# Second MLP by seven products of 256 tokens for eight, with weight sums made in HBM: one change to a hybrid SSD / HGRN2 trunk

## The chip, the cores and the metric

The kernel runs on one core of a Trainium2 chip. Its time is the device time of one launch in microseconds (us), and the median of three runs is what counts. Engines are named as the profile names them: PE (TensorE matmuls), PEld (its weight loads), DVE (VectorE), ACT (ScalarE), POOL (GpSimd) and SP (SyncE). Each engine works through its own instruction queue in order.

## What is computed

Two layers over 512 tokens of width 1024, all in float32. Layer 0 mixes tokens by a Mamba-2 SSD, layer 1 by HGRN2. Behind each mixer stand a layer norm, an MLP with a squared ReLU and 4096 hidden units, a second layer norm and a gate on a per-layer input:

```
x = layer_norm(alpha * x + mixer(x))
h = square(relu(x @ w1))            # 512 x 1024 by 1024 x 4096
x = layer_norm(alpha * x + h @ w2)  # 512 x 4096 by 4096 x 1024
x = x + gate(x, p)
```

Only the MLP of layer 1 ("MLP 1") is computed in another way by the change. MLP 0, the gate of layer 0 and the HGRN stage between the two MLPs keep their arithmetic.

## The kernel before

Every float32 matmul is made of three: each operand is split into a high part in float32r and the rest, and `mm3` (L119 to L122) issues high by high, high by low and low by high. So each weight piece of 128 x 1024 goes through four steps: a DMA into `raw` (3 buffers) or `r` (8 buffers), a cast on ACT into `whi` (L113), a subtraction on DVE into `wlo` (L116), and 24 matmuls. `whi` and `wlo` have six buffers each. `unit()` does the first three steps for a piece from HBM, with SP issuing the load; `split()` does the cast and the subtraction for a piece that is in SBUF already.

The first half of an MLP makes 32 hidden tiles of 128 units by 512 tokens. `hidden(g)` makes 8 of them for each of four groups g: 24 matmuls of 128x512 into a bank `pj`, a ReLU from PSUM (L587) and a square (L589) on ACT. After each four tiles `half_blocks` makes seven operand blocks (`b8`, `blk`: four blocks and four signed sums) by adds on DVE, casts on ACT (L307) and subtractions on DVE (L308).

The second half is already done by seven products for eight (Strassen's scheme in Winograd's form): `block_product` cuts a group's part of w2 into 2 x 2 blocks, and each `product` is 24 matmuls of 128x512, first those of one bank (c = 0), then those of the other. The banks are `py` (two) and `pj`, and each is drained into `acc` by DVE (L377). Four of the seven products use sums of weight blocks. `weight_sums` makes them in SBUF: eight loads on POOL's queue (L329) and eight DVE adds of 128x1024 (L336, L339, L340, L344) for each group. In the last group of an MLP the products go p1, p7, p6, p4, p5, p2, p3, and the layer norm of each 128 tokens follows on its last drain.

`PERIODS` orders tiles (T) and products (Q); the tile framework's scheduler then sets the order of each engine's queue from priorities and its own estimates. `SUMS` is how far ahead of their place in the program the loads and adds of weight sums are ranked. The stage behind MLP 0 and its gate ("values", 740 to 790 us) uses `weight_sums` as well, with the same `r` buffers. `last_gate` at the end uses four more sums in `r`.

Of the kernel before, what the change touches and what calls it, by code (L numbers as in the profile page):

```python
# [15 lines left out]
P = 128  # L16
# [15 lines left out]
PERIODS = ("TTTTTTTT",) + 3 * ("TTQTQTQTQTQTQTQ",) + ("QQQQQQQ",)  # L32
SUMS = (60, 300, 300, 300)
# [11 lines left out]
def trunk(ctx: ExitStack, tc, a):  # L45
# [30 lines left out]
    bufs = dict(ssd=dict(two, xs=4, sz=4, y=2, xdt=2, ecs=2, ss=2), mlp0=mlp, hgrn=dict(two, xs=4, sz=4, cv=4, y=2, pv=2, btok=2, sc=2, scb=2, qd=2), mlp1=mlp)  # L76
# [149 lines left out]
    turned_last = []  # L226

# [3 lines left out]
    def transpose_split(src, dst, c, apart, keep=None):  # L231

        sl = slice(c * P, (c + 1) * P)
        for q in range(2):
# [50 lines left out]
    def norm(i, keep=None):  # L285
# [9 lines left out]
        return h_s, chunk, lambda c: transpose_split(acc[:, c, :], h_s, c, c == 3 and i % 2 == 0, keep), sums  # L295
# [4 lines left out]
    def half_blocks(blk, z0, z1, p):  # L300
# [11 lines left out]
        nc.vector.tensor_add(a22, a21, a22)  # L312
        put("a12", a12)
        nc.vector.tensor_sub(a21, a11, a21)
        nc.vector.tensor_sub(a11, a22, a11)
        nc.vector.tensor_sub(a12, a12, a11)
# [30 lines left out]
    def block_product(w, blk, lead, first, after=None, turns=None, sums=None, low=None):  # L347

        t1, t2, t3, t4 = weight_sums(w, lead, after=low)
# [3 lines left out]
        def product(x, f, name, start, i, j, turns=None):  # L355
            us = [split(v) if f in (t1, t2, t3, t4) else unit(v) for v in f]
# [3 lines left out]
            for c in range(2):  # L360
# [10 lines left out]
                with tc.high_priority(offset=SOON if after else 0):  # L371
                    if after and f in (w[1][0], t1, t4, w[1][1]):
                        nc.vector.tensor_tensor_reduce(
                            d, ps, d, 1.0, 0.0, ALU.add, ALU.add, sums[:, 2 - 2 * i + c, j : j + 1]
                        )
                    elif (i, j) in seen:
                        nc.vector.tensor_add(d, ps, d)  # L377
                    else:
                        nc.vector.scalar_tensor_tensor(d, d, ALPHA, ps, ALU.mult, ALU.add)
# [9 lines left out]
        for f in (p1, p7, p6, p4, p5, p2, p3) if after else (p1, p2, p6, p7, p5, p4, p3):  # L389
            f()  # L390
# [6 lines left out]
    def last_gate(wp, wg, h_s, p_s, kept, turned):  # L397

        t3, t1, t2, t4 = (tmp("r", [P, 1024]) for _ in range(4))
# [158 lines left out]
    def mlp_and_gate(layer, h_s, last):  # L558
# [5 lines left out]
        def hidden(g):  # L564
# [5 lines left out]
            for p in range(2):  # L570
                tiles = [4 * (2 * g + r) + 2 * p + i for r in range(2) for i in range(2)]
# [892 lines left out]
```

## Time and profile before

| | |
|---|---|
| time, three runs | 1413.84, 1412.04, 1412.05 us; median 1412.05 us |
| span of the profiled execution | 1409.6 us; its own time is not listed apart from the three runs |
| granted TensorE clock | 1.00 in every stage |
| SSD mixer | 0 to 380 us |
| MLP 0 and its gate | 380 to 740 us |
| values, HGRN and its output | 740 to 1020 us |
| MLP 1 and its gate | 1020 to 1410 us |

A row of the timeline reads: start in us, length in us, engine, line, operation, output<-inputs with buffer numbers left out, shapes, count; behind it in brackets the idle time of that engine ahead of the row and what ended it. A matmul's length is modelled and overlaps the next one; the step from start to start is what it costs. A row of the stages gives, for a stretch, the busy time of PE, PEld, DVE, ACT and POOL with their counts, the granted clock, the mean share of the 16 DMA engines in use, and GB/s.

### The profile page before, as it was taken

What the parts mean: (1) busy time and instruction counts of PE and PEld (TensorE: products, weight loads), DVE (VectorE), ACT (ScalarE), POOL (GpSimd) and SP (SyncE); (2) the same over time, 40 slices, a digit from 0 to 9 for tenths busy, and PEclk for the clock granted to TensorE, in tenths of its full rate; (3) what the DMA queues carried; (4) which work ended last, traced back from release to release, by engine and by line L of the source; (5) the groups of instructions that cost most, each with busy time, mean ns of one, the idle gap of its engine ahead of it and who ended that gap; (6) DMA issues with size and microseconds to landing.
All of it is one profiled execution on the core that took longest, in us unless ns stands there. A gap on an engine that the chain in (4) does not pass through costs nothing.

```text
span 1409.6 us, 20400 instructions
## 1 busy us (share of the span) xinstructions
PE 1404.3 (100%) x8001; PEld 1168.1 (83%) x8001; DVE 1069.1 (76%) x1778; ACT 763.6 (54%) x1156; POOL 45.8 (3%) x92
## 2 busy tenths in 40 slices
PE   9999999999999999999999999999999999999998
PEld 7888888888988888888888888888898888888887
DVE  7989688698977668677986577678785867667795
ACT  7766465573354444545555547655555454544573
POOL 0000000001000000000000000000100000000100
PEclk9999999999999999999999999999999999999999
DMA  8433333234433444345621421222443444444731
GB/s 313 135 117 120 106 120 110 85 100 156 141 113 127 157 131 152 129 142 178 209 90 49 134 91 61 76 87 96 150 135 105 147 137 148 144 137 159 202 106 60
DMA packets 50399, 181.69 MB, mean 129 GB/s; under 512 B 5632, under 2 KB 6400, under 8 KB 50176
## 3 DMA queue, kind: packets, MB, share of 16 engines
q1 hardware_dynamic: 38784, 138.45, 29.6%
q0 software_dynamic: 11520, 41.95, 9.2%
q8 instruction: 63, 1.03, 0.3%
q14 instruction: 32, 0.26, 0.1%
HBM read 177.16 MB, written 2.16 MB: 127 GB/s over the span
## 4 chain that ended last, share of the span: by engine, by line
PE 99%; DMA 0%; DVE 0%; issue 0%; DVEq 0%
PE pj L120 25%; PE pj L121 25%; PE pj L122 25%; PE py L120 5%; PE py L122 5%; PE py L121 5%; PE py L906 1%; PE pt L238 1%; PE py L1175 1%; PE pm L923 1%; PE pm L871 1%; PE py L1301 1%; PE pt L859 0%; PE py L1303 0%; PE py L1240 0%; PE py L832 0%
## 5 line engine op out<-in xcount | busy, mean ns | idle before, releaser
L113 ACT CAST whi<-raw 128x1024 fp32r<-128x1024 f32 x218 | 228.8, 1050 | 333.2 <-PE pj L121 243.6
L120 PE MATMUL pj<-b,whi 128*128 128x512 f32 (+1 forms) x990 | 378.6, 383 | 0.0
L122 PE MATMUL pj<-b,wlo 128*128 128x512 f32 (+1 forms) x990 | 376.8, 381 | 0.0
L121 PE MATMUL pj<-b,whi 128*128 128x512 f32 (+1 forms) x990 | 376.6, 381 | 0.0
L116 DVE TENSOR_TENSOR wlo<-raw,whi 128x1024 fp32r<-128x1024 f32 x218 | 265.4, 1221 | 129.4 <-ACT whi L113 128.2
L121 PEld LDWEIGHTS pj<-b,whi 128*128 128x128 f32 x990 | 186.4, 188 | 34.6 <-issue 0.9
L122 PEld LDWEIGHTS pj<-b,wlo 128*128 128x128 f32 x990 | 186.3, 188 | 34.5
L120 PEld LDWEIGHTS pj<-b,whi 128*128 128x128 f32 x990 | 186.1, 188 | 34.0
L122 PE MATMUL pj<-whi,b 128*128 128x512 f32 x520 | 204.1, 392 | 0.0
L120 PE MATMUL pj<-whi,b 128*128 128x512 f32 x508 | 202.1, 398 | 0.0
L121 PE MATMUL pj<-wlo,b 128*128 128x512 f32 x508 | 199.2, 392 | 0.0
L113 ACT CAST whi<-r 128x1024 fp32r<-128x1024 f32 x76 | 80.0, 1053 | 68.5 <-PE pj L122 39.4
L122 PEld LDWEIGHTS pj<-whi,b 128*128 128x128 f32 x520 | 97.7, 188 | 20.1
L120 PEld LDWEIGHTS pj<-whi,b 128*128 128x128 f32 x508 | 95.5, 188 | 19.1 <-ACT b L1322 0.3
L121 PEld LDWEIGHTS pj<-wlo,b 128*128 128x128 f32 x508 | 95.5, 188 | 18.7 <-issue 0.2
L116 DVE TENSOR_TENSOR wlo<-r,whi 128x1024 fp32r<-128x1024 f32 x76 | 92.5, 1220 | 19.6 <-ACT whi L113 19.1
L122 PE MATMUL py<-whi,b 128*128 128x512 f32 x260 | 101.3, 390 | 0.0
L121 PE MATMUL py<-wlo,b 128*128 128x512 f32 x248 | 96.6, 389 | 0.0
L120 PE MATMUL py<-whi,b 128*128 128x512 f32 x248 | 96.4, 390 | 0.0
L329 POOL DMA_DIRECT2D r<-in_w x64 | 34.0, 532 | 1098.8 <-DVE wlo L116 544.3
L122 PEld LDWEIGHTS py<-whi,b 128*128 128x128 f32 x260 | 48.8, 188 | 10.2
L800 DVE SCALAR_TENSOR_TENSOR cv<-pj,cst,cv 128x509 f32<-128x509 f32 (+2 forms) x66 | 48.9, 746 | 10.6 <-ACT cv L797 9.8
(368 smaller groups left out, 1943.5 us busy)
## 6 DMA issues: line engine op xcount, KB each, us to landing
raw<-in_w SPq DMA_DIRECT2D x112, 512.0 KB, 3.3
r<-in_w POOLq DMA_DIRECT2D x64, 512.0 KB, 3.8
raw<-in_wssd SPq DMA_DIRECT2D x36, 512.0 KB, 3.9
a<-csd SPq DMA_DIRECT2D x16, 512.0 KB, 4.1
raw<-in_wso SPq DMA_DIRECT2D x16, 512.0 KB, 3.3
raw<-in_whq SPq DMA_DIRECT2D x16, 512.0 KB, 3.4
raw<-in_wg SPq DMA_DIRECT2D x15, 512.0 KB, 4.0
raw<-in_whvg SPq DMA_DIRECT2D x14, 512.0 KB, 3.4
```

The lines of the kernel that those rows point to most:

```text
L113: nc.scalar.copy(hi[:, :n], f)
L116: nc.vector.tensor_sub(lo[:, :n], f, f32(hi[:, :n]))
L120: nc.tensor.matmul(out, sh, mh, start=start, stop=False, **kw)
L121: nc.tensor.matmul(out, sh, ml, start=False, stop=False, **kw)
L122: return nc.tensor.matmul(out, sl, mh, start=False, stop=stop, **kw)
L238: nc.tensor.transpose(pt[:, j * P : (j + 1) * P], src[:, k * P : (k + 1) * P], ident)
L329: queue.dma_start(t[i][u], src)
L800: nc.vector.scalar_tensor_tensor(cv[:, d:], ps[:, : T - d], convw[:, i, k : k + 1], cv[:, d:], ALU.mult, ALU.add)
L871: nc.tensor.matmul(pst_[:, c * P : (c + 1) * P], btok[:, c, :], xw[:, c].rearrange("p h q -> p (h q)"), start=True, stop=True)
L906: mm = nc.tensor.matmul(yds[0][64 * r : 64 * r + 64, sl], xdt[:, 2 * c + r, :], m[:, r, sl], start=True, stop=True)
L923: mm = nc.tensor.matmul(yo[:, c * P : (c + 1) * P], pv[:, c - 1].rearrange("p h q -> p (h q)"), cm[:, c * P : (c + 1) * P], start=True, st ...
L1175: nc.tensor.matmul(pcs[r][bs, at : at + n], kk[r][:, ts], qs, start=True, stop=True)
```

## The change

In the first half of MLP 1, 28 of the 32 tiles are made in 14 pairs, by the same scheme of seven products for eight. `pair()` does one: the 1024 inputs are cut in two halves, the two tiles are the two output halves, and the tokens are cut into 2 x 256. Each of the seven products is 12 matmuls of 128x256, so a pair takes 84 of them where two tiles took 48 of 128x512. The partial results go through PSUM into `z` by three copies on ACT and three adds on DVE, each 256 wide. The sums of the tokens are made once, by `token_sums`: four DVE adds, four ACT casts and four DVE subtractions of 128x1024, from a float32 copy `whole` that eight further ACT copies make while the layer norm's output is transposed. The four tiles made first stay as they were.

The sums of weight blocks, of w1 for the pairs and of w2 for MLP 1's second half, are formed in HBM ahead of time. `block_sums` lists 56 DMAs of 512 KB for s1 and 32 of 1 MB for s2, half of them copies from HBM to HBM and half of them adding copies, all on POOL's queue. `add_blocks` issues them during MLP 0 behind drains of `acc` and during HGRN behind matmuls ("pace"). In MLP 1 the 32 loads on POOL's queue and the 32 DVE adds are gone; the sums come by `unit` as plain weights do. A pair takes three and a half pieces of 128x1024 through load, cast and subtraction where two tiles took two. `PAIRS` orders the halves of products (q), products (Q) and parts of pairs (T); `last_gate` uses four buffers `tb` for its sums.

```diff
+PAIRS = ("TTTTTTTTTT",) + 3 * ("TTqqTTqqTqTTqqTqTqTqqTqTqq",) + ("QQQQQQQ",)
...
+    def block_sums():
...
+            yield small(o1, b21, False)
+            yield small(o3, b21, False)
+            yield small(o1, b22, True)
+            yield small(o3, b11, True)
+            yield small(o2, o1, False)
+            yield [(t1, wb, False)]
+            yield small(o2, b11, True)
...
+    def add_blocks(n=1):
+        for _ in range(n):
+            for out, src, add in next(steps, ()):
+                dma = nc.gpsimd.dma_start(out, src, **(dict(accum_op=ALU.add, max_dma_last_dim=8192) if add else {}))
+                tc.add_manual_dep(
+                    dma.ins, paced[0].ins.name, mybir.DependencyInfo(mybir.DependencyClass.Sync, mybir.DependencyReason.DATA), reason="pace"
+                )
...
+                if whole is not None:
+                    nc.scalar.copy(whole[c // 2][:, q, :, c % 2 * P : (c % 2 + 1) * P], v)
...
+    def pair(w1, q, h_s, ts, z, pz):
...
+        def product(ps, w, cs, x, start):
+            for k in range(4):
+                ks = slice(cs.start + k * P, cs.start + (k + 1) * P)
+                mm3(ps, w[0][:, ks], w[1][:, ks], *x(k), start and k == 0, k == 3, skip_group_check=True)
+        plain = unit(w1[2 * q])
+        product(xy[:, first], plain, low, part(0, first), True)
+        nc.scalar.copy(z[:, 0, first], xy[:, first])
+        product(zz[:, first], plain, high, part(4, first), True)
+        nc.vector.tensor_add(z[:, 0, first], zz[:, first], z[:, 0, first])
+        us = unit(both(0))
+        product(zz[:, second], us, low, ts[2], True)
+        nc.scalar.copy(z[:, 1, second], zz[:, second])
+        product(xy[:, first], us, high, ts[1], False)
+        nc.scalar.copy(z[:, 1, first], xy[:, first])
+        nc.scalar.activation(z[:, 0, first], z[:, 0, first], AF.Relu)
+        yield
...
+                if op == "Q" and not last and g < 4:
+                    add_blocks(2 if g > 1 else 1)
...
-                mm3(pss[c], *x, hi[:, ks], lo[:, ks], j + k == 0, j == 3 and k == 1)
+                paced[0] = mm3(pss[c], *x, hi[:, ks], lo[:, ks], j + k == 0, j == 3 and k == 1)
...
+    add_blocks(64)
+    whole = [mk(b8, [P, 2, 4, 256], "b8") for _ in range(2)]
+    h_s, *after = norm(2, whole=whole)
```

Up to the last group of MLP 0, and again from its gate to MLP 1, PE's matmuls stand in the same order as before, but for one place in the values stage and a few transposes of the norm between. The queues of the other engines move as follows. Lines of the kernel before and after differ: L329 is now L382, L336/L339/L340/L344 are L389/L392/L393/L397, L116 is L117, L377 is L435.

POOL, before: the eight loads of the sums of MLP 0's last group (`r_926` to `r_933`) stand right behind those of the group ahead of it.

```order
L329 DMA r_845_5012<-in_w2_0 128x1024 [waits DMASW6_49,DVE_49]
L329 DMA r_846_5013<-in_w2_0 128x1024 [waits DMASW7_49,DVE_49]
L329 DMA r_932_5543<-in_w2_0 128x1024 [waits DMASW0_49,DVE_49]
L329 DMA r_926_5537<-in_w2_0 128x1024 [waits DMASW1_49,DVE_49]
L329 DMA r_928_5539<-in_w2_0 128x1024 [waits DMASW2_49,DVE_49]
```

POOL, after, at the same loads: 21 DMAs of the sums stand between the two groups, of which these are the last.

```order
L270 DMA s2<-in_w2_1 16x16384 [waits DMASW5_49,DVE_49]
L270 DMA s1<-s1 128x2x512 [waits DMASW6_49,DMASW3_49]
L270 DMA s1<-s1 128x2x512 [waits DMASW7_49,DMASW4_49]
L382 DMA r_932_5589<-in_w2_0 128x1024 [waits Activation_49]
L382 DMA r_926_5583<-in_w2_0 128x1024 [waits Activation_49]
L382 DMA r_928_5585<-in_w2_0 128x1024 [waits DMASW2_49,Activation_49]
```

The loads now stand behind DMAs that wait for a drain on DVE and for one another.

DVE, before, at the end of MLP 0's third group: the adds into `r_926` to `r_933` stand 15 to 42 rows further up, and the first two subtractions from them are here, ahead of the last operand blocks.

```order
L116 TENSOR_TENSOR wlo_939_5571<-raw_937_5567,whi_938_5569 128x1024 [waits DMAHW2_49,Activation_49]
L308 TENSOR_TENSOR b8_828_4938<-b_857_5072,b8_828_4938 128x512 [waits Activation_49]
L377 TENSOR_TENSOR acc_2_99<-pj_888_5272,acc_2_99 128x512
L116 TENSOR_TENSOR wlo_943_5603<-r_926_5537,whi_942_5601 128x1024 [waits Activation_49]
L116 TENSOR_TENSOR wlo_945_5607<-r_927_5538,whi_944_5605 128x1024 [waits PE_49,Activation_49]
L377 TENSOR_TENSOR acc_2_99<-py0_855_5044,acc_2_99 128x512 [waits PE_49]
L308 TENSOR_TENSOR b8_827_4937<-b_897_5366,b8_827_4937 128x512 [waits Activation_49]
```

DVE, after, some ten rows later in its queue: `py1_941` is the second bank of the last group's first product p1, and `blk_830` (its next product, p7) is multiplied by the pieces `r_926` and `r_927`.

```order
L435 TENSOR_TENSOR acc_2_99<-py1_856_5071,acc_2_99 128x512
L736 TENSOR_TENSOR b_924_5578<-raw_925_5579,a_923_5577 128x1024 [waits DMAHW7_49,DVE_49,Activation_49]
L435 TENSOR_TENSOR acc_2_99<-py1_941_5620,acc_2_99 128x512 [waits PE_49]
L389 TENSOR_TENSOR r_926_5583<-r_926_5583,r_932_5589 128x1024 [waits DMASW1_49,DMASW0_49]
L392 TENSOR_TENSOR r_932_5589<-r_932_5589,r_928_5585 128x1024 [waits DMASW2_49,DVE_49]
L117 TENSOR_TENSOR wlo_943_5649<-r_926_5583,whi_942_5647 128x1024 [waits Activation_49]
L393 TENSOR_TENSOR r_928_5585<-r_926_5583,r_928_5585 128x1024 [waits DVE_49]
L389 TENSOR_TENSOR r_927_5584<-r_927_5584,r_933_5590 128x1024 [waits DMASW4_49,DMASW3_49]
```

All eight adds and the first four subtractions now stand behind the drain of p1's second bank.

DVE, before, in the values stage: `pt_1068` holds transposed outputs, and `py1_1069` the last bank of MLP 0's gate.

```order
L630 TENSOR_TENSOR b8_1003_5890<-pt_1068_6287,b8_1001_5888 128x4x128 [waits PE_49,Activation_49]
L116 TENSOR_TENSOR wlo_1097_6389<-raw_1095_6385,whi_1096_6387 128x1024 [waits DMAHW3_49,Activation_49]
L116 TENSOR_TENSOR wlo_1101_6429<-raw_1099_6425,whi_1100_6427 128x1024 [waits DMAHW4_49,Activation_49]
L116 TENSOR_TENSOR wlo_1104_6435<-raw_1102_6431,whi_1103_6433 128x1024 [waits DMAHW5_49,Activation_49]
L116 TENSOR_TENSOR wlo_1107_6470<-r_1073_6341,whi_1106_6468 128x1024 [waits Activation_49]
L116 TENSOR_TENSOR wlo_1109_6474<-r_1074_6342,whi_1108_6472 128x1024 [waits Activation_49]
L664 TENSOR_TENSOR sg_1071_6303<-py1_1069_6295,sg_1071_6303 128x512 [waits Activation_49]
```

DVE, after, at the same place: the last four of the stage's eight adds on `r` are seen here.

```order
L392 TENSOR_TENSOR r_1080_6394<-r_1080_6394,r_1076_6390 128x1024 [waits DMASW3_49,DVE_49]
L801 TENSOR_TENSOR acc_2_99<-sg_1067_6305,acc_2_99 128x512 [waits DVE_49]
L117 TENSOR_TENSOR wlo_1097_6435<-raw_1095_6431,whi_1096_6433 128x1024 [waits DMAHW3_49,Activation_49]
L117 TENSOR_TENSOR wlo_1101_6475<-raw_1099_6471,whi_1100_6473 128x1024 [waits DMAHW4_49,Activation_49]
L117 TENSOR_TENSOR wlo_1104_6481<-raw_1102_6477,whi_1103_6479 128x1024 [waits DMAHW5_49,Activation_49]
L393 TENSOR_TENSOR r_1076_6390<-r_1074_6388,r_1076_6390 128x1024 [waits DVE_49]
L397 TENSOR_TENSOR r_1077_6391<-r_1077_6391,r_1075_6389 128x1024 [waits DMASW4_49]
L397 TENSOR_TENSOR r_1078_6392<-r_1078_6392,r_1076_6390 128x1024 [waits DMASW5_49,DVE_49]
L765 TENSOR_TENSOR b8_1003_5936<-pt_1068_6333,b8_1001_5934 128x4x128
```

The read of `pt_1068`, which PE's next transposes wait for, and that of `py1_1069`, which the first matmuls of a product wait for, now stand behind these adds; seven adds were put between 748 and 763 us of the trace of before, and one ahead of that.

ACT, after, in MLP 1 where one group ends and the next begins: `b_1572` is the last `z` of the old group, `pj_1636` the first bank of the next pair.

```order
L672 ACTIVATE b_1572_10252<-pj_1601_10451 128x256 [waits PE_49]
L673 ACTIVATE b_1572_10252<-b_1572_10252 128x1024 [waits Activation_49]
L353 CAST b8_1514_9881<-b_1572_10252 128x512 [waits Activation_49]
L353 CAST b8_1513_9880<-b_1572_10252 128x512
L114 CAST whi_1651_10795<-raw_1650_10793 128x1024 [waits DMAHW1_49,PE_49]
L353 CAST b8_1515_9882<-b_1572_10252 128x512 [waits DVE_49]
L353 CAST blk_1518_9885<-b_1520_9887 128x512 [waits PE_49]
L353 CAST blk_1517_9884<-a_1571_10251 128x512 [waits DVE_49]
L114 CAST whi_1654_10801<-raw_1653_10799 128x1024 [waits DMAHW2_49]
L653 COPY a_1634_10685<-pj_1636_10687 128x256 [waits PE_49]
```

The copy of the next pair's first partial result, which PE must have before it adds to that bank, stands behind this work; before, a tile had no such copy.

More of the change, by code (lines that the diff above doesn't have):

```diff
@@ L283, in out_project, with norm @@
                     out_part(units, 4, xs, c, h, first, scale)
-    def norm(i, keep=None):
+    def norm(i, keep=None, whole=None):
         gb = ln_params(i)
@@ L293, in chunk, with half_blocks @@
                 layer_norm(i, c, gb, sums)
-        return h_s, chunk, lambda c: transpose_split(acc[:, c, :], h_s, c, c == 3 and i % 2 == 0, keep), sums
-    def half_blocks(blk, z0, z1, p):
+        return h_s, chunk, lambda c: transpose_split(acc[:, c, :], h_s, c, c == 3 and i % 2 == 0, keep, whole), sums
+    def half_blocks(blk, z0, z1, p, plus):
         ks = slice(2 * p, 2 * p + 2)
@@ L560, in mlp_and_gate @@
+    def mlp_and_gate(layer, h_s, last, whole=None):
         w1, w2 = a[f"w1_{layer}"], a[f"w2_{layer}"]
@@ L570, in hidden @@
             for p in range(2):
+                if whole is not None and (g or p):
+                    zs = [mk(w4, [P, 2, T], "ab"[r]) for r in range(2)]
+                    pairs = [pair(w1, 4 * g + 2 * r + p, h_s, ts, zs[r], ((pst, "pt"), (psm, "pm"))[r]) for r in range(2)]
+                    order = (0, 1, 0, 1, 0, 1) if g == 0 else (0, 0, 0, 1, 1, 1)
+                    for at, n in enumerate(order):
+                        next(pairs[n])
+                        if at == 5:
+                            half_blocks(blocks[g], *zs, p, True)
+                        yield
+                    continue
                 tiles = [4 * (2 * g + r) + 2 * p + i for r in range(2) for i in range(2)]
```

131 lines of the change are left out of this document (105 added, 26 removed).

## The prediction

> **What bounds the kernel now.** I read the page first, for the shares and the chain of waits.
>
> ```profile
> span 1409.6 us, 20400 instructions
> PE 1404.3 (100%) x8001; PEld 1168.1 (83%) x8001; DVE 1069.1 (76%) x1778; ACT 763.6 (54%) x1156; POOL 45.8 (3%) x92
> PE 99%; DMA 0%; DVE 0%; issue 0%; DVEq 0%
> ```
>
> PE is never idle and carries the whole chain, so a matmul saved is time saved, and any wait that is given to PE is time lost. The sum is made against the span of 1409.6 us; the median of the runs, 1412.05, is 2.45 us longer, and I add that at the end. The timeline of PE then gives what a matmul costs, by the steps from start to start, for 256 wide (first tiles of MLP 1) and 512 wide.
>
> ```profile
> 1025.75 0.28 PE L121 MATMUL pj<-b,whi 128*128 128x256 f32 x1
> ...
> 1027.43 0.28 PE L120 MATMUL pj<-b,whi 128*128 128x256 f32 x1
> 661.73 0.39 PE L120 MATMUL py<-whi,b 128*128 128x512 f32 x1
> ...
> 663.09 0.39 PE L120 MATMUL pj<-whi,blk 128*128 128x512 f32 x1
> ...
> 676.83 0.39 PE L120 MATMUL pj<-whi,b 128*128 128x512 f32 x1
> ```
>
> The first two are 14 steps apart: 0.120 us each. From 661.73 to 663.09 there are six: 0.227 us each. The last row is the spot at which MLP 0's last group has done its products p1, p7 and p6; I use it below. Third, the stages:
>
> ```profile
> 420.00:740.00 320.00, 320.00 (x1436) 264.66 (x1435) 241.82 (x298) 160.04 (x210) 16.95 (x32) 1.00 0.44 146
> 780.00:1020.00 240.00, 240.00 (x2236) 197.35 (x2235) 169.43 (x475) 141.34 (x318) 5.51 (x12) 1.00 0.31 102
> 1020.00:1060.00 40.00, 40.00 (x253) 36.14 (x252) 35.16 (x42) 22.86 (x35) 0.00 (x0) 1.00 0.38 122
> 1140.00:1220.00 80.00, 80.00 (x355) 66.26 (x354) 55.67 (x65) 38.14 (x48) 4.24 (x8) 1.00 0.45 144
> ```
>
> DVE is the next engine, with 70% in MLP 1's steady part and 88% at its start; DMA has room.
>
> **The gain.** Two tiles cost 48 x 0.227 = 10.90 us, a pair 84 x 0.120 = 10.08 us: 0.82 us saved, 14 times, 11.4 us. A product of half the width saves an eighth of the work and pays the part of a step that does not halve (0.120 against 0.1135) on all of it. The granted clock is 1.00 everywhere, so no stage owes a different step.
>
> For the same step the Trainium skill, "TensorE: Matmul & The Clock Gate", section "Back-to-back issue gap", gives N / 2.4 + 2.5 ns for the isolated gap, some 109 ns for 256 wide and 216 for 512; by that estimate a pair would save 1.19 us and all of them 16.6, and the sum below would be 5.2 us lower. The rows here disagree (120 and 227 ns), so I keep the rows.
>
> **MLP 0's last group: the largest loss.** PE's work there is not changed, but DVE's queue is. I walk it with these rows.
>
> ```profile
> 636.64 1.22 DVE L344 TENSOR_TENSOR r<-r,r 128x1024 f32<-128x1024 f32 x1 [0.23 <-DMA r<-in_w]
> 637.78 0.68 DVE L377 TENSOR_TENSOR acc<-py,acc 128x512 f32<-128x512 f32 x1
> 651.76 1.22 DVE L116 TENSOR_TENSOR wlo<-r,whi 128x1024 fp32r<-128x1024 f32 x1
> 655.99 1.22 DVE L116 TENSOR_TENSOR wlo<-r,whi 128x1024 fp32r<-128x1024 f32 x1 [3.01 <-ACT whi L113]
> 658.46 1.28 DVE L308 TENSOR_TENSOR b<-b,b 128x512 fp32r<-128x512 f32 x2
> 659.66 0.69 DVE L312 TENSOR_TENSOR b<-a,b 128x512 f32<-128x512 f32 x1
> 668.60 2.56 DVE L116 TENSOR_TENSOR wlo<-r,whi 128x1024 fp32r<-128x1024 f32 x2
> 671.07 0.68 DVE L377 TENSOR_TENSOR acc<-pj,acc 128x512 f32<-128x512 f32 x1
> ```
>
> Before, the last add was done at 637.8, the first subtractions from the sums ran at 651.8 and 656.0, and PE took the first at 663.09 and the second six matmuls later, at 664.45: 10 and 7 us in hand. A 512-wide operation costs 0.60 us (658.46 to 659.66 for two), a 1024-wide one 1.14 (636.64 to 637.78), or 1.24 with its wait (668.60 to 671.07 for two). In the changed queue fourteen 512-wide operations run from 658.46, and the last of them, the drain that frees p1's second bank, ends at 658.46 + 14 x 0.60 = 666.9. Before, PE filled that time with p7; now p1's second bank comes first, runs from 667.0 to 667.0 + 12 x 0.227 = 669.7, and its drain ends at 670.3. Only then come twelve 1024-wide operations, eight adds and four subtractions: 670.3 + 12 x 1.14 = 684.0. PE picks up each piece as it is made, and has 16 matmuls left behind the last: 684.0 + 16 x 0.227 = 687.6, against 676.83. That is 10.8 us. With 1.24 for each it is 12.0; if the first two pieces alone were late and the others overlapped (667.0 - 663.1 at the bank, 669.7 to 673.8 at the first piece), 8.0. I take 11, for the walk has all its rows from this very place, and keep 8 to 13. Behind it the two banks of the next products and the layer norm move along by the same time; nothing there waits for longer, since DVE is as late as PE is.
>
> The loads are not what costs: in the changed queue of POOL they wait for a drain at about 608 us and for eight DMAs of sums, which leaves 60 us until DVE wants them. The scheduler's place for the adds costs, and no cover is left, since p7 and p6 both use the sums.
>
> **The values stage.** The same eight adds come late a second time.
>
> ```profile
> 740.64 1.22 DVE L708 TENSOR_TENSOR blk<-blk,blk 128x1024 f32<-128x1024 f32 x1
> 745.99 0.69 DVE L664 TENSOR_TENSOR sg<-py,sg 128x512 f32<-128x512 f32 x1 [4.13 <-ACT sg L663]
> 747.93 1.22 DVE L682 TENSOR_TENSOR b<-blk,b 128x1024 fp32r<-128x1024 f32 x1
> 753.28 0.69 DVE L664 TENSOR_TENSOR sg<-py,sg 128x512 f32<-128x512 f32 x1 [4.14 <-ACT sg L663]
> 759.72 2.58 DVE L116 TENSOR_TENSOR wlo<-r,whi 128x1024 fp32r<-128x1024 f32 x2
> 762.22 0.69 DVE L664 TENSOR_TENSOR sg<-py,sg 128x512 f32<-128x512 f32 x1
> 762.96 0.50 PE L120 MATMUL py<-whi,b 128*128 128x512 f32 x1
> ```
>
> One add fits in the idle 4.13 us ahead of 745.99 and three in those ahead of 753.28. The other four have no cover: from 753.28 DVE has four 512-wide operations, four adds and five subtractions ahead of the gate's last read of PSUM: 753.28 + 4 x 0.60 + 9 x 1.14 = 765.9, where it ended at 762.9. PE's product at 762.96 waits for that read: 3.0 us, or 4.0 with 1.24 for each. I take 3.5, and keep 2 to 5 (a transposition ahead of it waits too, but inside the same time).
>
> **MLP 1.** Bytes and engines suffice. In a group of four pairs (78 us of PE) 30 pieces (four of them half as long) pass through `whi` and `wlo` instead of 22; DVE loses eight adds and gains six subtractions and twelve 256-wide adds, ACT six casts and twelve copies, which makes some 59 and 50 us of 78 (the stage's 55.67 and 38.14 of 80, with 0.4 for a 256-wide operation, an estimate from the 0.60 of 512). What shrinks is the time in hand: six `whi` buffers serve 30 uses in 78 us (15.7 us round) where they served 22 in 82 (22 us). The shortest way from a freed buffer to a weight ready for PE is a cast and a subtraction:
>
> ```profile
> 655.86 0.59 ACT L587 ACTIVATE b<-pj 128x512 f32<-128x512 f32 x1
> 656.48 1.07 ACT L589 ACTIVATE b<-b 128x1024 f32<-128x1024 f32 x1
> 657.58 1.14 ACT L307 CAST b<-b 128x512 fp32r<-128x512 f32 x2
> 667.49 1.05 ACT L113 CAST whi<-r 128x1024 fp32r<-128x1024 f32 x1
> ```
>
> 1.05 + 1.22 = 2.3 us, so inside a group I expect no wait. Where a group ends, ACT has a ReLU, a square, six casts of 512 (0.57 each) and two of 1024 ahead of the next pair's first copy: 0.4 + 1.1 + 6 x 0.57 + 2 x 1.05 = 7.0 us and some waits on DVE between, against 2 x 2.72 + 2 x 1.44 = 8.3 us of PE work: a wait of 0 to 1.5 us at the copy and as much at the next, three times. At the start, four token sums and four subtractions (8 x 1.14 = 9.1 us on DVE) take the place of eight adds, and each transposition waits for one more ACT copy of 0.57. No row of before shows this stage; from below it costs nothing (every piece in time), from above 15 us (three group ends at 3 us, and the start at 6, what its added copies, casts and subtractions come to beyond the idle 5 us of DVE there). I take 7, from the walk of the group ends (1.5 each) and 2.5 at the start.
>
> **Costed at nothing.** HGRN's order is unchanged; its PE order has the new semaphores, but no new wait. The DMAs of the sums move 61.9 MB beside its weight loads.
>
> ```profile
> q1 hardware_dynamic: 38784, 138.45, 29.6%
> q0 software_dynamic: 11520, 41.95, 9.2%
> raw<-in_w SPq DMA_DIRECT2D x112, 512.0 KB, 3.3
> ```
>
> 180.4 MB took 38.8% of the span, 330 GB/s while the engines run. The sums need 188 us at that rate, 281 if an adding DMA (half of them) counts twice for reading its target, in some 470 us from 526 on. That is 0.40 to 0.60 on top of 0.44 and 0.31. A load of 3.3 us may become two or three times as long; the weights have seven us and more in hand.
>
> **The sum.** -11.4 + 11 + 3.5 + 7 = +10.1: a span of 1419.7, a time of 1422.
>
> **The rivals.**
> - Faster: the walk of MLP 0's last group is too pessimistic, because the fourteen operations ahead of the drain start earlier or run beside one another, so that p7's first piece is late by only some 5 us and the rest follows in time; the values stage costs 2 and MLP 1 nothing. -11.4 + 5 + 2 = -4.4, 1407.7. It decides from the point where the three losses come to under 8.6. For it: DVE was idle for some 8 us between 641 and 658. Against it: the adds stand behind the drain of PE's own p1 in DVE's queue, which they can't pass.
> - No change: lower ends everywhere, 8 + 2 + 0 = 10, gives -1.4, 1410.7.
> - DMAs run full: with adds counted twice MLP 0's second half has 0.44 + 0.60 = 1.04. From a share over 1 on, weights come late: 4% of 470 us is 19 us more, 1441. For it: half of the sums are adds and each waits for the one ahead. Against it: HGRN has 0.31, and takes half of them. The Trainium skill, "DMA: Bandwidth & Descriptors", section "Issuing engines are not separate DMA queues", has all queues interleave on the same 16 engines, which is this rival's premise; no run so far shows both loads together.
> - The change doesn't do what it says: the pairs' steps are longer than 0.120 since a pair loads as many weights for half the columns. PEld is busy 83% now. If a step were 0.130, a pair would cost 10.92 and the gain would be gone: 1433. Against it: the first tiles of before do just this for 15 rows at 0.120.
>
> **Chances.** The forecast's own case (the three losses between 14 and 33, so a time of 1415 to 1434) 0.60; faster 0.19; no change 0.14; DMAs full 0.05; no gain 0.02. The range 1405 to 1434 leaves out the lower half of the faster case, the two last ones and what lies above the forecast's own. A measurement here tells 0.2%, 2.8 us, from no change: faster 0.19, same 0.14, and slower the other three, 0.67.
>
> **What would show it.** Right: PE rows of 128x256 stepping by 0.120 in MLP 1; PE idle behind DVE `wlo` and ACT `whi` at about 663 to 685 us for 11 us, and behind DVE at 760 to 767 for 3.5; single waits of about a us at three places in MLP 1. Wrong: no idle PE at 663 to 685, weights waiting for DMAs in HGRN, or waits all through MLP 1's groups, where I have none.

## The result, and the profile after

The changed kernel takes 1449.28 us (median of four runs, 1448.22 to 1453.77) against 1412.43 for the kernel before (four runs): a ratio of 1.0269, 95% interval 1.0252 to 1.0286. It is slower, as forecast, but by 37 us and not by 10; the time lies above the range. First the page of the profile after: span, engines, the chain of waits, and the two kinds of DMA queue (packets, MB, share of the 16 engines).

```profile
span 1446.6 us, 21844 instructions
PE 1412.2 (98%) x8505; PEld 1189.2 (82%) x8505; DVE 1082.4 (75%) x1824; ACT 806.1 (56%) x1252; POOL 104.7 (7%) x148
PE 41%; DVE 5%; DMA 5%; ACT 2%; issue 1%; ACTq 0%; DVEq 0%; SPq 0%
q1 hardware_dynamic: 47424, 166.24, 34.2%
q0 software_dynamic: 21376, 88.09, 24.3%
```

PE no longer carries the whole chain: DMA, DVE and ACT have entered it. (The chain is followed back to 667.6 us only; its shares are of the whole span and come to 54%. PE's busy time still reads 1412, in part since a matmul at a slower clock counts as busy for longer.) POOL's queue moves 88.09 MB in place of 41.95 and takes 24.3% of the engines' time in place of 9.2%. By stage (PE, PEld, DVE, ACT and POOL busy, granted clock, DMA share, GB/s):

```profile
580.00:640.00 60.00, 58.60 (x259) 48.19 (x258) 37.92 (x47) 29.73 (x39) 12.22 (x15) 1.00 0.91 237
640.00:700.00 60.00, 52.81 (x211) 41.88 (x210) 43.49 (x52) 23.69 (x29) 13.71 (x19) 0.91 0.96 278
700.00:760.00 60.00, 52.87 (x246) 42.75 (x245) 40.98 (x63) 29.54 (x51) 6.93 (x11) 0.94 0.80 247
900.00:1000.00 100.00, 100.00 (x1087) 82.53 (x1086) 72.13 (x229) 61.33 (x144) 20.69 (x24) 1.00 0.92 238
1140.00:1220.00 80.00, 79.78 (x505) 71.86 (x504) 59.76 (x78) 49.33 (x73) 0.00 (x0) 1.00 0.57 184
1300.00:1340.00 40.00, 37.58 (x214) 33.01 (x213) 24.29 (x31) 20.41 (x28) 3.49 (x5) 0.96 0.81 247
```

PE loses time where the engines' share is 0.91, 0.96 and 0.80 (MLP 0's end and its gate) and again past 1300, but none at 0.92 in HGRN: a full set of DMA engines costs nothing by itself. (Not for a share of 1 either: in single stretches of 6 us in HGRN it reads up to 1.20, from 966 to 972, and PE is busy throughout.) The waits of PE, largest first (us in total, how often, the longest):

```profile
PE pt L282 <- DVE acc L225: 7.5, 2, 5.9
PE py L121 <- DVE acc L435: 7.0, 5, 2.8
PE pj L121 <- ACT whi L114: 3.0, 1, 3.0
PE pj L121 <- DVE b L668: 2.4, 1, 2.4
PE py L121 <- DVE sg L799: 2.1, 1, 2.1
```

Next I set the start of each matmul beside that of the same one before (PE's order is the same but for a part of MLP 0's last group, a few transposes and MLP 1, where I count back from the end). How far the changed kernel is behind grows like this:

| stretch of the changed kernel | added, us | forecast |
|---|---|---|
| start | 0.5 | 0 |
| MLP 0's third group (at 594) | 1.7 | 0 |
| MLP 0's last group (660 to 695) | 12.4 | 11 |
| MLP 0's layer norm and gate (705 to 736) | 9.1 | 0 |
| values (786 to 794) | 5.4 | 3.5 |
| HGRN, then MLP 1 up to its last products, the gain included | 0.5 | -4.4 |
| last products and gate (from 1335) | 7.1 | 0 |
| sum | 36.7 | 10.1 |

**MLP 0's last group.** DVE's timeline follows the forecast's walk (the drain of p1's second bank forecast to end at 670.3, the adds from then to 684):

```profile
667.56 0.68 DVE L435 TENSOR_TENSOR acc<-py,acc 128x512 f32<-128x512 f32 x1
...
672.84 0.69 DVE L435 TENSOR_TENSOR acc<-py,acc 128x512 f32<-128x512 f32 x1 [3.46 <-PE py L123]
673.44 1.21 DVE L389 TENSOR_TENSOR r<-r,r 128x1024 f32<-128x1024 f32 x1
...
685.04 4.62 DVE L117 TENSOR_TENSOR wlo<-r,whi 128x1024 fp32r<-128x1024 f32 x4
```

The drain of p1's second bank ends at 673.44, and the adds stand behind it, as the order said. That is 3.1 us later than walked, of which 2.2 are the lag that the kernel brought along (0.5 and 1.7 in the table). The operations ahead of the drain ended some 1 us earlier than that, and the bank itself took 4.5 us (668.29 to 672.84) instead of 2.7. PE's rows show why:

```profile
668.29 0.80 PE L121 MATMUL py<-whi,b 128*128 128x512 f32 x1 [2.82 <-DVE acc L435]
668.89 0.63 PE L122 MATMUL py<-wlo,b 128*128 128x512 f32 x1
669.32 0.63 PE L123 MATMUL py<-whi,b 128*128 128x512 f32 x1
...
671.72 0.40 PE L123 MATMUL py<-whi,b 128*128 128x512 f32 x1
```

After a wait of 2.82 us the steps are 0.43 us instead of 0.227 for some 3 us, and then back to normal. The granted clock (the last number but two) says the same:

```profile
664.00:668.00 4.00, 1.48 (x7) 0.90 (x5) 4.00 (x8) 2.28 (x4) 0.00 (x0) 1.00 1.04 232
668.00:672.00 4.00, 3.71 (x10) 2.94 (x11) 1.37 (x2) 0.00 (x0) 0.00 (x0) 0.57 1.03 184
```

**The norm and the gate.** The chain of waits here names two loads of the gate's weights:

```profile
698.37 10.59 DMA raw<-in_wg
...
710.14 1.22 DVE wlo L117
...
715.79 9.63 DMA raw<-in_wp
...
726.58 1.23 DVE wlo L117
```

Before, such loads took 3.3 us (`in_wg`, median) and 4.3 (`in_wp`). DVE's subtraction of each stands ahead of layer-norm work in its queue, and PE's transposes wait for that (the 5.9 us at `pt`). DVE's timeline shows it for another such weight; L224 and L225 are the layer norm:

```profile
707.53 1.23 DVE L117 TENSOR_TENSOR wlo<-raw,whi 128x1024 fp32r<-128x1024 f32 x1 [4.53 <-ACT whi L114]
...
711.48 1.28 DVE L224 SCALAR_TENSOR_TENSOR acc<-acc,lnmv,a 128x1024 f32<-128x1024 f32 x1
...
717.55 2.47 DVE L225 SCALAR_TENSOR_TENSOR acc<-acc,lnrs,b 128x1024 f32<-128x1024 f32 x2
```

The cast at 706.45, for which DVE waits here, had itself kept ACT waiting 5.56 us for its load. Late weights hold up work that does not use them. The 1.7 us at 594 are of the same kind: DVE stands idle for 4.79 us, up to 587.48, for the cast of a late weight, and the drain that PE wants comes behind eight more operations.

**The end.** The chain from 1335, with a raw buffer's round of load, cast (ACT) and subtraction (DVE), three times over:

```profile
1335.65 6.22 DMA raw<-s
...
1341.89 1.07 ACT whi L114
...
1342.98 1.14 DVE wlo L117
...
1346.57 6.59 DMA raw<-s
...
1357.90 5.75 DMA raw<-s
```

The sums of the last group, which before stood ready in eight `r` buffers, now pass through three `raw` ones.

### The profile page after: what moved, and what is told of

Read it like the earlier page. It is cut to its first block, busy times and chain, and to the rows that moved or that the text cites. A ratio compares the mean times of both kernels' runs of the same rounds, so it can differ in the third digit from the quotient of the medians.

```text
span 1446.6 us, 21844 instructions
## 1 busy us (share of the span) xinstructions
PE 1412.2 (98%) x8505; PEld 1189.2 (82%) x8505; DVE 1082.4 (75%) x1824; ACT 806.1 (56%) x1252; POOL 104.7 (7%) x148
## 3 DMA queue, kind: packets, MB, share of 16 engines
q0 software_dynamic: 21376, 88.09, 24.3%
HBM read 251.09 MB, written 65.08 MB: 219 GB/s over the span
## 4 chain that ended last, share of the span: by engine, by line
PE 41%; DVE 5%; DMA 5%; ACT 2%; issue 1%; ACTq 0%; DVEq 0%; SPq 0%
PE pj L121 9%; PE pj L122 9%; PE pj L123 9%; PE py L121 2%; PE py L122 2%; PE py L123 2%; DVE wlo L117 2%; DMA raw<-s 2%; DMA raw<-in_w 1%; ACT whi L114 1%; DMA raw<-in_wg 1%; PE py L1310 1%; PE pt L121 1%; PE pm L121 1%; DMA raw<-in_wp 1%
## 5 line engine op out<-in xcount | busy, mean ns | idle before, releaser
L117 DVE TENSOR_TENSOR wlo<-raw,whi 128x1024 fp32r<-128x1024 f32 (+1 forms) x278 | 330.5, 1194 | 195.4 <-ACT whi L114 194.1
L114 ACT CAST whi<-raw 128x1024 fp32r<-128x1024 f32 (+1 forms) x278 | 285.2, 1028 | 319.6 <-PE pj L122 149.4
L121 PE MATMUL pj<-b,whi 128*128 128x512 f32 (+1 forms) x878 | 323.3, 369 | 3.1 <-DVE b L668 2.4
L122 PE MATMUL pj<-b,whi 128*128 128x512 f32 (+1 forms) x878 | 321.4, 366 | 0.0
L123 PE MATMUL pj<-b,wlo 128*128 128x512 f32 (+1 forms) x878 | 321.0, 366 | 0.0
L121 PEld LDWEIGHTS pj<-b,whi 128*128 128x128 f32 x878 | 165.5, 189 | 29.9 <-DVE b L668 2.8
L122 PEld LDWEIGHTS pj<-b,whi 128*128 128x128 f32 x878 | 165.9, 189 | 26.5 <-issue 0.9
L123 PEld LDWEIGHTS pj<-b,wlo 128*128 128x128 f32 x878 | 165.7, 189 | 25.8
L270 POOL DMA_DIRECT2D s<-in_w x66 | 61.1, 986 | 335.9 <-issue 149.0
L114 ACT CAST whi<-r 128x1024 fp32r<-128x1024 f32 x40 | 41.6, 1051 | 43.7 <-PE pj L123 18.4
L121 PEld LDWEIGHTS py<-whi,b 128*128 128x128 f32 x248 | 47.4, 191 | 20.8 <-DVE acc L435 9.1
L117 DVE TENSOR_TENSOR wlo<-r,whi 128x1024 fp32r<-128x1024 f32 x40 | 48.1, 1217 | 14.2 <-ACT whi L114 14.2
L123 PEld LDWEIGHTS py<-whi,b 128*128 128x128 f32 x260 | 49.5, 190 | 10.4
## 6 DMA issues: line engine op xcount, KB each, us to landing
s<-in_w POOLq DMA_DIRECT2D x16, 1024.0 KB, 11.9
```

The source lines that it names most:

```text
L114: nc.scalar.copy(hi[:, :n], f)
L117: nc.vector.tensor_sub(lo[:, :n], f, f32(hi[:, :n]))
L121: nc.tensor.matmul(out, sh, mh, start=start, stop=False, **kw)
L122: nc.tensor.matmul(out, sh, ml, start=False, stop=False, **kw)
L123: return nc.tensor.matmul(out, sl, mh, start=False, stop=stop, **kw)
L270: dma = nc.gpsimd.dma_start(out, src, **(dict(accum_op=ALU.add, max_dma_last_dim=8192) if add else {}))
```

## Experiments

My theory after the result: the sums' DMAs cost some 29 us, through their place in DVE's queue (12) and through full engines (the rest); the pairs themselves gain 11 in MLP 1 and lose as much in waits there, and the last products lose 7 for want of buffers. Rivals: the pairs cost more than they show; the order alone costs all of it; or the order costs nothing and only late loads do.

**1. The pairs without the sums' DMAs.** The 88 DMAs are left out, and MLP 1 reads plain pieces of w1 and w2 in the places of the sums.

```diff
-        for _ in range(n):
+        for _ in range(0):
...
-        both = lambda n: s1[q][:, n : n + 2, :].rearrange("p s n -> p (s n)")
+        both = lambda n: w1[2 * q + n // 2]
```

> The changed kernel without the 88 DMAs of the sums: MLP 1 reads plain pieces of w1 and w2 of the same sizes where it read sums, so its output is not the reference's. DVE's order up to MLP 1 is then that of the kernel before. My theory (36.8 us of loss = 29 between 590 and 790 us from the sums' DMAs, by DVE's late adds and by full DMA engines; 1 at HGRN's end; MLP 1 even, its gain of 11.2 eaten by small waits; 7 in the last products and the gate): the 29 go, 7 stay, 1420 us. Rival A (the last 7 are a late effect of the sums' DMAs too): 1413. Rival B (a part of the 29 comes from elsewhere, such as the clock): above 1425.

1418.61 us, ratio 1.0045 (1.0025 to 1.0064). 30.7 us of the 36.8 go with the DMAs. The lag is 1.35 up to HGRN and -1.7 where the last products begin, so the pairs do gain 3 us up to there; then the last products and the gate lose 8.9, where the changed kernel loses 7.1:

```profile
1290.00:1320.00 30.00, 23.95 (x121) 19.32 (x119) 15.93 (x21) 13.22 (x18) 4.83 (x7) 1.00 0.93 281
1310.48 6.61 DMA raw<-in_w
```

(A stage, and a row of its chain of waits.) So the end's loss belongs to MLP 1's own loads, and even with the sums for nothing the kernel is not faster.

**2. The sums' DMAs without the pairs.** The kernel before with the 88 DMAs and the same places for them; MLP 1 as it was.

> The kernel before with the 88 DMAs of the sums added at their places, MLP 1 as before (the sums are made and not used). DVE's order up to MLP 1 is that of the changed kernel. Theory: the loss up to HGRN alone, 29 us, so 1441 to 1442. Rival (the loss needs the pairs, for example their loads waiting for the sums): 1413 to 1420.

1445.08 us, ratio 1.0233 (1.0203 to 1.0263), 3 above the theory. The lag is 28.6 through HGRN (29.1 in the changed kernel), and grows by 6.7 behind it, mainly at two waits: 1.7 us from 1024 on, while sums still run, and 2.7 from 1133 on with a halved clock behind it. The second ends on an add of weight sums that stands late in DVE's queue, and the changed MLP 1 has no such adds. DMA shares in MLP 1's start, of this kernel:

```profile
1030.00:1060.00 30.00, 30.00 (x177) 25.60 (x176) 23.91 (x47) 14.44 (x31) 6.72 (x10) 1.00 0.86 229
1060.00:1090.00 30.00, 30.00 (x174) 26.49 (x173) 17.67 (x21) 17.99 (x26) 2.47 (x4) 1.00 0.91 288
```

The sums are not done when HGRN is; the last of them goes out at 1076 here and at 1069.65 in the changed kernel. I had not seen that: their chain, in which each adding DMA waits for the one ahead of it, runs over into MLP 1.

**3. The order alone.** The kernel before, with no DMA added; only the eight adds of weight sums of MLP 0's last group stand behind the drain of p1's second bank.

```diff
+            if defer and f is p1:
+                adds(drains[-1])
```

> The kernel before with one thing moved: the eight weight adds of MLP 0's last group stand behind the drain of the first product's second bank in DVE's queue, as in the changed kernel (all eight in a row, then the subtractions). No DMA is added, loads are where they were. Theory (the place in DVE's queue is enough): 11 to 16 us slower, 1424 to 1428, with PE idle between 665 and 690 us and half the clock for about 3 us behind each wait of some 3 us. Rival (that wait in the changed kernel came from loads landing late): 1412 to 1416.

1429.24 us, ratio 1.0121 (1.0091 to 1.015). A lag of some 16 us arises between 663 and 685 and nowhere else:

```profile
PE py L120 <- ACT whi L113: 3.3, 1, 3.3
PE pj L120 <- ACT whi L113: 3.0, 1, 3.0
640.00:700.00 60.00, 48.62 (x197) 38.36 (x196) 44.47 (x53) 23.70 (x28) 4.24 (x8) 0.89 0.42 149
```

(Two waits of PE, and the stage.) The engines' share is 0.42 there and no load is late, so the place in DVE's queue is enough for this term. It costs more than the 12.4 of the changed kernel: here all eight adds run ahead of the first subtraction, and there one subtraction runs after every two or three adds.

**4. The loads on the other queue.** The changed kernel, with the loads of `weight_sums` issued by SP instead of POOL. DVE's order becomes that of before up to MLP 1.

```diff
-    def weight_sums(w, lead, after=None, queue=nc.gpsimd):
+    def weight_sums(w, lead, after=None, queue=nc.sync):
```

> The changed kernel with the loads of weight sums of MLP 0 and of the values stage on SP's queue instead of POOL's, so that no DMA of s1 or s2 stands ahead of them; DVE's order up to MLP 1 is then that of the kernel before, the sums' DMAs stay. Theory (DVE's late adds cost 12.4 + 5.4 by themselves, full DMA engines 11): 1431. Rival (the DMA engines are full and everything that is loaded between 590 and 790 us is late whatever the queue): 1443 to 1449. Rival the other way (without the late adds nothing waits): 1421.

1463.16 us (two runs, 1457.93 and 1468.39), ratio 1.0361 (1.0273 to 1.0449): neither theory. The adds are back in their place, but their loads are not there. From the chain of waits:

```profile
649.64 12.53 DMA r<-in_w
668.18 11.15 DMA raw<-in_w
704.14 13.60 DMA raw<-in_w
```

Beside POOL's sums these loads take 11 to 14 us, though SP issues them, and in one queue `r` and `raw` hold each other up: from 600 to 720 SP's `r` loads wait 32 us in all for a buffer, with `raw` loads behind them. This agrees with the Trainium skill, "DMA: Bandwidth & Descriptors", section "Issuing engines are not separate DMA queues", by which another issuer saves only issue time. So mending the order doesn't help while the loads are late. The two runs also tell the causes apart at MLP 0's norm and gate: this one, with the order of before, loses 10.8 us there, and experiment 3, with late adds and no added DMA, loses nothing. The values stage, whose adds are back in their place, loses nothing here.

**5. The last group's sums in other buffers.** The eight pieces go, on POOL's queue, into the four token-sum buffers, free by then.

```diff
+                for t in (t3, t2, t4, t1):
+                    held.append(tmp("tb", [P, 2, 1024]))
+                    for u in range(2):
+                        nc.gpsimd.dma_start(held[-1][:, u], t[u])
```

> The changed kernel, but the eight pieces of weight sums of MLP 1's last group are loaded on POOL's queue into the four token-sum buffers, which are free by then, instead of passing through the three raw buffers on SP's queue. Same bytes, same casts and subtractions. Theory (at the end each raw buffer goes round load, cast, subtraction in about 8.5 us, 2.8 us for a piece against PE's 2.7, so the ring of three sets the pace): the 7.1 us lost in the last products and the gate shrink to 0 to 2, time 1442 to 1444. Rival (the DMA engines are the limit there, 0.8 busy, or the loads start too late): 1448 to 1450.

1445.48 us, ratio 1.0237 (1.0221 to 1.0252): 3.8 less. The end loses 0.9 instead of 7.1, so the way through the ring of three was its cause; but eight loads at once fill the engines just ahead of it (share 1.01), and PE waits 3.0 us and goes on at half the clock:

```profile
1330.00:1345.00 15.00, 12.01 (x64) 10.23 (x63) 7.81 (x9) 7.36 (x10) 2.12 (x4) 0.89 1.01 398
```

**6. A fourth raw buffer in MLP 1.**

```diff
+            raw = tmp("rx", [P, 1024]) if "rx" in phase[2] and turn[0] % 4 == 0 else mk(raws, [P, 1024], "raw")
```

> The changed kernel with a fourth raw buffer in MLP 1 and the last gate (every fourth piece goes into it; its room comes from the gate's two sigmoid buffers, which take token-sum buffers instead). Theory (three raw buffers are what holds MLP 1: SP waits for a raw buffer's subtraction 80 times, and 30 pieces a group pass through the three where there were 14, with eight r buffers beside them): 3 to 6 of the some 11 us of small waits in MLP 1 and 4 to 7 of the 7 us at the end go, time 1437 to 1443. Rival (the pace is set by ACT, DVE or the six whi buffers): within 2 of 1449.

1458.17 us (four runs, 1447.93 to 1460.91), ratio 1.0302 (1.026 to 1.0345): a miss, 9 slower in the median. The new buffer lies in the space of MLP 1, which HGRN's norm must leave first: its first load goes out at 1059.02, lands 9.85 us later, and its cast holds ACT for 6.52 us ahead of the norm's copies:

```profile
1068.89 1.04 ACT L117 CAST whi<-rx 128x1024 fp32r<-128x1024 f32 x1 [6.52 <-DMA rx<-in_w]
```

PE waits 8.3 us there, and the last products and the gate still lose some 6, by other waits. Whether a buffer that is free from the start would help stays open.

**7. No sums in MLP 0.** The DMAs go out behind SSD's projections and in HGRN.

```diff
-                if op == "Q" and not last and g < 4:
-                    add_blocks(2 if g > 1 else 1)
```

> The changed kernel, but none of the 88 DMAs of sums is issued in MLP 0: they go out behind projections of the SSD mixer (DMA share 0.40 there) and in HGRN. Theory (MLP 0's loss comes from DMAs that stand ahead of its own loads and from full engines in its second half): the 28 us that are lost up to HGRN go and 0 to 4 come in SSD, time 1419 to 1424. Rival (88 DMAs of 62 MB cost PE the same wherever they run, since every load beside them takes longer): the loss moves to SSD and HGRN, 1435 to 1450.

1423.05 us, ratio 1.0073 (1.0058 to 1.0088). MLP 0, its gate and the values lose nothing; this is the stage that had PE at 52.81:

```profile
640.00:700.00 60.00, 60.00 (x267) 49.46 (x266) 50.95 (x69) 33.09 (x44) 4.26 (x8) 1.00 0.57 198
```

SSD runs at a share of 0.72 to 0.95 and loses at most 2 us. So the same DMAs cost 29 us in one place and 2 in another. Nearly all that is left, 10.5 us, is lost in the last products and the gate.

**8. All three together**, experiments 5, 6 and 7.

> All three together: sums' DMAs in SSD and HGRN, the last group's sums through the token-sum buffers, a fourth raw buffer in MLP 1. If the three losses are separate, they add: 1449 - 28 - 6 - 4 = 1408 to 1414, faster than the kernel before by up to 0.3%. Rival (with more loads in flight the engines' share rises to full in MLP 1 and at the end, so the second and third give nothing): 1418 to 1422.

1420.82 us, ratio 1.0059 (1.0044 to 1.0074): they don't add, since each of 5 and 6 brings the new wait seen above (3.8 us from 1306 on and 3.3 from 1032 on).

**9. The loads of the last group spread.** Experiments 5 and 7, and six of the eight loads wait for the last drain of the group ahead.

```diff
+                        if t is not t3:
+                            pace(dma)
```

> Sums' DMAs in SSD and HGRN as before, and the last group's sums through the token-sum buffers, but with the three raw buffers of the changed kernel, and six of the eight loads wait for the last drain of the group ahead, so that they don't run all at once beside the weights that PE needs next (all at once the engines were full, 1.01 from 1330 to 1345, and PE waited 3.4 us there). Theory (what is lost at the end is a burst of loads that comes too late or too thick): of the 13 us lost there and at MLP 1's start without it, 3 to 6 stay, time 1413 to 1417. Rival (whatever the order, the loads of the last 100 us are too many): 1420 to 1424.

1420.37 us, ratio 1.0056 (1.0044 to 1.0069): a miss, at the lower end of the rival's range. The products are served now (under 2 us lost in all), and the wait has gone on to the last layer norm:

```profile
PE pt L284 <- DVE acc L225: 5.1, 1, 5.1
```

It is MLP 0's gate over again: a load of gate weights that takes 7.72 us, whose subtraction stands ahead of the norm in DVE's queue. POOL's queue, with the sums' loads and the last gate's own chain of loads, copies and adds, has 65.5% of the engines' time from 1320 to 1350.

**10. The last gate's sums made in HBM too**, in SSD (eight DMAs more there, four plain loads at the end).

> As the one before, and the four sums of weights for the last gate, too, are made in HBM during SSD (eight DMAs more there), so that four plain loads take the place of a chain of eight, half of them adding, beside MLP 1's last products. Theory: that chain takes some 46% of the DMA engines' time in 1300 to 1330 for 3 MB, and without it the loads that PE waits for land in 4 us instead of 6 to 7; 1 to 4 us less than the one before, 1410 to 1415. Rival (its loads were already out of the way): the same as the one before within 1 us.

1434.23 us, ratio 1.015 (1.0124 to 1.0177): right at the end and wrong in the sum. The end loses 2.4 instead of 8.8 (from the last group's first product on). But eight DMAs more push the chain of sums to about 1105, and MLP 1's start pays over 20:

```profile
1030.00:1060.00 30.00, 25.47 (x176) 23.56 (x175) 20.82 (x24) 19.37 (x28) 5.93 (x7) 0.94 0.95 248
1060.00:1090.00 30.00, 25.29 (x182) 24.46 (x181) 18.18 (x27) 17.03 (x30) 2.73 (x4) 0.89 0.92 240
```

**11 and 12. The same, with sums issued earlier.** First seven steps in MLP 0's second period and five ahead of HGRN; then eight in the first period, a dozen in the second, and none ahead of HGRN (the edit shown).

```diff
+                if not last and g < 2 and op == "TQ"[g]:
+                    add_blocks(1 + g * (at % 3 > 0))
```

> As the one before (gate sums in HBM too), but some twelve of the steps of sums are issued earlier: seven behind products of MLP 0's second period, where the engines have room (0.60 from 420 to 500 in the changed kernel, no loss up to 589), and five ahead of HGRN's first background work (in the last kernels POOL issues none from 787 to 849). PE's and ACT's orders are the same. Theory (its loss of 23 us at MLP 1's start is only that the sums' chain was still running till about 1105, with the engines at 0.95 and 0.92; its end lost 5, not 10): the chain ends by 1040, 3 to 6 us lost at the start and 4 to 6 at the end, time 1410 to 1416. Rival (the steps added in MLP 0 push its later loads back as in the changed kernel, or the gate sums cost elsewhere): 1420 or more.

1417.03 us, ratio 1.0031 (1.0019 to 1.0043), 1 above the theory: 3 us lost by the sums ahead of HGRN, 4.3 in a wait from 999 on (6 with the longer steps behind it), and the chain done by about 1030.

> As the one before, but the early steps are placed otherwise: none ahead of HGRN (PE waited 3 us near 697 to 704 in the last kernel, and 4.7 at 999, where sums' DMAs still ran), eight behind tiles of MLP 0's first period (engines at 0.34 from 360 to 420 there) and some eleven behind products of its second. Theory: the sums end in HGRN, well before 1000; of the 9.3 us that the last kernel's profiled run is behind, 5 to 8 go, time 1410 to 1414, level with the kernel before or up to 0.2% faster. Rival (eleven steps crowd MLP 0's second and third period, where loads of sums share POOL's queue with its own): 1417 to 1425.

1413.49 us (eleven runs) against 1412.48, ratio 1.0003 (0.9994 to 1.0012): level with the kernel before, and 36 us better than the change. Its page and stages:

```profile
PE 1400.0 (99%) x8505; PEld 1183.0 (84%) x8505; DVE 1081.7 (77%) x1824; ACT 806.2 (57%) x1252; POOL 110.9 (8%) x160
420.00:500.00 80.00, 80.00 (x354) 66.26 (x354) 47.35 (x58) 39.00 (x49) 17.07 (x22) 1.00 0.91 254
640.00:700.00 60.00, 60.00 (x268) 49.48 (x267) 51.95 (x71) 32.96 (x44) 4.31 (x8) 1.00 0.59 200
1300.00:1340.00 40.00, 37.21 (x169) 30.10 (x168) 31.49 (x41) 21.28 (x25) 5.36 (x10) 1.00 0.66 232
```

MLP 0's second period runs at a share of 0.91 and PE loses nothing; that its loads have more time in hand is the likely reason, but I did not measure it. The profiled run is 2.4 us behind at the end of SSD and 2.7 at the end of all, so MLP 1 with the gate comes out even: the gain of 11.2 goes into some 1.5 at its start, 5 to 6 in its steady part, a wait of 2.1 just ahead of the last products, and 2.3 in these and the gate.

## Why the prediction was wrong in size

The sum was 26.6 us short. Of these, 10.8 lie in MLP 0's third group, norm and gate, which were costed at nothing; 7.1 in the last products and the gate, which had no term; 4.9 in MLP 1; and 3.8 in the rest.

- **The gain** was right: 14 x (48 x 0.227 - 84 x 0.120) is 11 us, and 256-wide steps are 0.120 (631 of 672 from 1140 to 1300). The rival of longer steps falls.
- **MLP 0's last group** was right: 12.4 for 11 (8 to 13), by the place named. Experiment 3 shows the place alone suffices. The walk left out the clock, which cost 1.8 us in p1's second bank alone: "the granted clock is 1.00 everywhere" held before, when PE never waited.
- **Values** were right in the mechanism and low in size: 5.4 for 3.5 (2 to 5). DVE's rows fit the walk (one add, then three, and four behind these), and PE's two waits come to 3.3 (1.11 and 2.15). Most of the rest is seven steps of 0.43 behind them, 1.4 us: the clock again. POOL's loads went out late (713 to 735, against 658 to 680 in experiment 9), but no row of DVE from 758 to 792 waits for one.
- **"Costed at nothing ... the weights have seven us and more in hand"** is the step that failed. The share of 0.40 to 0.60 on top of 0.44 was right (0.79 to 0.96 measured from 500 to 760), and so was "a load may become two or three times as long" (3.3 to 10.6). But time in hand was counted for the matmul that uses a weight. What was late was everything behind that weight's subtraction in DVE's queue: 9.1 us at the norm and gate, 1.7 at 594. The rival of full engines, at 0.05, had the right cause and a wrong rule (a share over 1, and then everywhere): below 1 it cost at two places, and at 0.92 in HGRN nothing, nor above 1 in single stretches there. Experiments 2, 3, 4 and 7 show it. (The 61.9 MB of the sums are 62.9: HBM written went from 2.16 to 65.08. That changes nothing here.)
- **The last products and the gate** were not in the sum at all: 7.1. I worked out the round of the six `whi` buffers and not that of the three `raw` ones: the last group's sums moved there from eight `r` buffers, and a round is 8.4 us (6.22 + 1.07 + 1.14), 2.8 for a piece against PE's 12 x 0.227 = 2.7 (a product's 24 matmuls take two pieces). Experiments 1 and 5 show where the loss comes from. The 2.8 against 2.7 alone makes 1.4 us for 14 pieces; that a ring without cover passes on every longer load (6.95 and 6.59 us here) is how I explain the rest, and it is not shown.
- **MLP 1's waits** came to 10 or 11 for 7, inside my 0 to 15, but not where I put them, at the group ends: 4.7 lie in the steady part (1085 to 1325), of which two dozen single steps of 0.22 to 0.27 instead of 0.12 make 2.8, nearly all by the first matmul of a product on token sums. What makes these longer stays open.
- **Sums that run over into MLP 1** I had not thought of; experiment 2 shows some 2 us of it with the old MLP 1, and experiment 10 over 20 with a longer chain. In the changed kernel itself it isn't separable from MLP 1's other waits.

## What to carry over

When a change adds transfers, cost each late load not by the matmul that needs it but by everything behind its cast and its subtraction in the engines' queues: place the transfers where those queues have slack (here a share of 0.91 of the DMA engines cost nothing in one period of MLP 0, and in its last two, its gate and the values the same sums cost 29 us). When operands move from one set of buffers to another, work out the round of the set that they join: load as long as it will then be, plus each operation on it, over the number of buffers. And look for the end of a chain of dependent DMAs: it stops when its last link has landed, not when the last one was written into the program.

## What the hardware showed

A wait of PE of some 3 us can halve its granted clock for the next 3 us or so (2.82 us at 668.29, then six steps of 0.43; 0.57 in 668 to 672): in the whole changed kernel the longer steps behind waits come to some 7 us. The length of the wait alone doesn't decide: in experiment 3 a wait of the same 2.82 us, at 666.72, is followed by steps of 0.23 and a clock of 1.00, and in experiment 6 one of 2.00 us, at 595.53, by seven steps of 0.43. In the runs here every wait over 4 us was followed by half the clock, and none under 1.9 us by itself; what decides between stays open. The Trainium skill, "TensorE: Matmul & The Clock Gate", Part 1, has half the clock after an idle window of about 3.4 us and 426.7 ns for 512 wide; the 0.43 agrees, and 2.00 and 2.82 us of idle time were enough here.

Copies and adds between HBM places landed 512 KB in 7.6 us (median of 42) and 1 MB in 11.9 us (16), beside other loads; POOL's plain loads of 512 KB took 8.8 us in the same kernel (32), so they do not land later than loads on the same queue. They take more of the engines, by this estimate: before, POOL's queue, with loads alone, took 9.2% of 1409.6 us for 41.95 MB, 3.1 us for each MB. After, it took 24.3% of 1446.6, 352 us; less 78 for 25.2 MB of loads, 274 us are left for the sums' 62.9 MB, 4.4 for each. The prediction has 281 if an adding DMA counts twice.
